# A two-layer hybrid trunk: first tiles and weights in a fixed order of need, keys and values tile by tile, the end-of-layer scaling on VectorE

## The chip, the cores and the metric

The kernel runs on one core of a Trainium2 chip. The metric is the time of one execution in microseconds (us) on the device; less is better. The text calls the engines as the profile does: PE (TensorE, matrix products), PEld (its weight loads), DVE (VectorE), ACT (ScalarE), POOL (GpSimd) and SP (SyncE, which issues the transfers). Each engine works through its own list of instructions in order, so an instruction that waits holds up everything behind it on its engine.

## What is computed

Two layers, each of this form, on x of 512 x 1024 in float32:

```
h    = rms_norm(x, g_pre)
proj = h @ w_in         # q_h, f_h, i_h, z_h (1024 each), q_a (1024), k_a, v_a (128 each), z_a (1024)
o_h  = hgrn2(q_h, f_h, i_h, lb)              # gated linear recurrence, 8 heads, state 128 x 128
o_h  = rms_norm(o_h, g_head) * silu(z_h)
q_a, k_a = rotary(q_a), rotary(k_a)          # 16 query heads, 2 key heads of 64
o_a  = sliding_window_attention(q_a, k_a, v_a, sinks) * silu(z_a)   # window 128
y    = concat(o_h, o_a) @ w_out              # 2048 -> 1024
x    = x + rms_norm(y, g_post)
```

## The kernel before

The tokens are four tiles of 128 (`NT`). Every projection is done with three products in a reduced-precision float format (`mm3`): each operand is split into a rounded part (`hi`) and the rest (`lo`), and a product is hi x lo, lo x hi and hi x hi, added in one PSUM tile.

Weights come in pieces of 128 x 512. SP loads a piece (`raw`, three buffers), ACT rounds it to `whi` (L169; `wkv` for the keys' and values' weights), and DVE takes the difference, `wlo` (L170). For every second piece of the slabs in `POOL_SLABS` and of the keys and values it is POOL that makes `wlo`. `w_conv` runs ahead of use by a count of pieces.

The projections are slabs of 512 columns, in a fixed order: `kv` (256 columns), `QA` and the next one (attention queries; the text calls the second QA+1), `IV` and so on, and at the end the output slabs up to `h1`. A slab is a row of units, each one PSUM tile with its steps over k (a step is one `mm3`, three matmuls). `step()` takes one step, in turn from one or two active units: when the only active one is half done, the next is begun beside it. Work that belongs to a later step is put into a list with `later(steps, key, fn)`, counted down by one at each step; `ensure(key)` runs it at once when a unit needs it. `merge` runs the streams of attention and recurrence between the steps.

At the start of a layer `pre_norm` makes each tile's mean square (ACT, L302), the inverse root `r` (one DVE and one POOL operation, `rstd2`, L280 and L282), `xn` (DVE, L306, two halves), eight transposes on PE (L311), and by `split_psum` the rounded part `hhi` (ACT, L267) and the rest `hlo` (DVE, L268). A `kv` unit's eviction copies its PSUM tile on ACT, rotates the keys on DVE at once, writes the values `vst`, and defers the key transposes by 16 steps. The QA evictions write `rot` with DVE (L378 to L385), POOL (L388, L389), ACT (L391) and DVE again; SP stores it as `stack` and loads it back as `qs`.

At the end of a layer (`final`, from L733 on) each half of `y` is added up on DVE (L719), squared on ACT (L745), its first half multiplied by g_post on POOL (L747, `y<-y,b`), the second on DVE (L750), then `r`, and `a` is the new x (L753, two halves). In layer 1 `pre_norm` of the next layer follows with `defer` of `DEFER` = 18 steps.

The order of instructions on each engine is made by a scheduler from the order in the code and from priorities (`tc.high_priority`); `pin` keeps an instruction in the place it was written.

Of the kernel before, what the change touches and what calls it, by code (L numbers as in the profile page):

```python
# [19 lines left out]
DEPTH = 2  # L20
# [17 lines left out]
LEAD = 4  # L38
POOL_SLABS = (QA,)
# [26 lines left out]
def hybrid_kernel(ctx: ExitStack, tc: tile.TileContext, x, wkv, win, wout, g_pre, g_post, lbp, ghead, sinks,  # L66
# [80 lines left out]
    def w_load(n):  # L147
        while state["raw"] < min(n, len(pieces)):
            i = state["raw"]
            src = pieces[i]  # L150
            t = wp.tile([P, 512], F32, tag="raw", name="raw", bufs=RAW_BUFS)
            nc.sync.dma_start(t.rearrange("p (a c) -> p a c", a=2) if len(src.shape) == 3 else t, src)
            raws[i] = t
            state["raw"] += 1

    def w_conv(n):
        w_load(n)
        while state["conv"] < min(n, len(pieces)):
# [5 lines left out]
            if i in kv_pieces:  # L164
                hi, lo = (big.tile([P, 512], F32R, tag="v", name="wkv", bufs=8) for _ in range(2))
            else:
                hi = wp.tile([P, 512], F32R, tag="whi", name="whi")
                lo = wp.tile([P, 512], F32R, tag="wlo", name="wlo")
            nc.scalar.copy(hi, v)  # L169
            (nc.gpsimd if i in on_pool and i % 2 else nc.vector).tensor_tensor(lo, v, hi.bitcast(F32), op=ALU.subtract)  # L170
            conv[i] = (hi, lo)
# [39 lines left out]
    def step():  # L211
        if not active or (len(active) == 1 and units and 2 * (len(active[0].ks) - active[0].i) <= len(active[0].ks)):
# [64 lines left out]
    def rstd2(ss):  # L277

        t = sm.tile([P, 1], F32, tag="s1", name="s1")
        nc.vector.scalar_tensor_tensor(t, ss[:, 0:1], EPS, ss[:, 1:2], op0=ALU.add, op1=ALU.add)  # L280
        r = sm.tile([P, 1], F32, tag="r1", name="r1")
        nc.gpsimd.tensor_tensor(r, t, mhalf[:, 0:1], op=ALU.pow)  # L282
        return r
# [12 lines left out]
    def pre_norm(tt, xt, g, hT, key, defer=0):  # L296

        ss = sm.tile([P, 2], F32, tag="ss", name="ss")
        xn2 = big.tile([P, 2, 512], F32, tag="q", name="xn", bufs=QB)
        for c in range(2):  # L300
            junk = tmp("u")
            nc.scalar.activation(junk, xt[c], AF.Square, scale=1.0 / 32.0, accum_out=ss[:, c:c + 1])  # L302
        r = rstd2(ss)
        for c in range(2):
            xn = xn2[:, c]
            nc.vector.scalar_tensor_tensor(xn, xt[c], r, g[c], op0=ALU.mult, op1=ALU.mult)  # L306

            def rest(c=c, xn=xn):
                o = sc()
                for j in range(4):  # L310
                    pin(nc.tensor.transpose(o[:, j * P:(j + 1) * P], xn[:, j * P:(j + 1) * P], ident))  # L311
                ov = o.rearrange("p (k t) -> p k t", k=4)
                sl = (slice(None), slice(4 * c, 4 * c + 4), slice(tt * P, (tt + 1) * P))
                split_psum(hT[0][sl], hT[1][sl], ov)

            later(defer, key if c == 1 else None, rest)
            if not defer:
                run_first()
# [5 lines left out]
    def layer(l, last):  # L324
# [4 lines left out]
        def kv_evac(tt, o):  # L329
# [10 lines left out]
            k4 = raw[:, 0:128].rearrange("p (v d) -> p v d", v=2)  # L340
            x1, x2 = k4[:, :, 0:32], k4[:, :, 32:64]
            cb = kcos[:, tt, :].unsqueeze(1).broadcast_to([P, 2, 32])
            sb = ksin[:, tt, :].unsqueeze(1).broadcast_to([P, 2, 32])
            kk = rk[:, 256:512].rearrange("p (v d) -> p v d", v=2)
            m = sm.tile([P, 4, 2, 32], F32, tag="km", name="km", bufs=1)
            nc.vector.tensor_tensor(m[:, 0], x1, cb, op=ALU.mult)
            nc.vector.tensor_tensor(m[:, 1], x2, sb, op=ALU.mult)
            nc.vector.tensor_tensor(m[:, 2], x2, cb, op=ALU.mult)
            nc.vector.tensor_tensor(m[:, 3], x1, sb, op=ALU.mult)
            nc.vector.tensor_tensor(kk[:, :, 0:32], m[:, 0], m[:, 1], op=ALU.subtract)  # L350
            nc.vector.tensor_tensor(kk[:, :, 32:64], m[:, 2], m[:, 3], op=ALU.add)
            nc.scalar.copy(kk[:, :, 64:128], kk[:, :, 0:64])
# [9 lines left out]
            later(16, ("k", l, tt), rest)  # L362
# [348 lines left out]
        def wo_stream(b, s, final=None):  # L711
            def evac(o, tt, ch):
# [4 lines left out]
                else:  # L717
                    with tc.high_priority(200 if final else 0):
                        nc.vector.tensor_tensor(yt[tt][:, ch], o, yt[tt][:, ch], op=ALU.add)  # L719
                if final is not None:  # L720
                    final(tt, ch)
# [10 lines left out]
        def final(tt, ch):  # L732
# [11 lines left out]
            junk = tmp("u")  # L744
            nc.scalar.activation(junk, y[:, ch], AF.Square, scale=1.0 / 32.0, accum_out=ss[:, ch:ch + 1])  # L745
            if ch == 0:
                nc.gpsimd.tensor_tensor(y[:, 0], y[:, 0], hT2["gpost"][0], op=ALU.mult)  # L747
# [38 lines left out]
    def x_tile(tt):  # L786
        t = halves("a") if tt < 2 else (lambda v: [v[:, 0], v[:, 1]])(big.tile([P, 2, 512], F32, tag="oy", name="x0", bufs=6))
        for c in range(2):
            nc.sync.dma_start(t[c], x[tt * P:(tt + 1) * P, c * 512:(c + 1) * 512])
        return t  # L790
# [6 lines left out]
    gpre = load_g(g_pre[0])  # L797
    w_load(1)
    for tt in range(1, NT):
        xts.append(x_tile(tt))  # L800
        w_load(1 + tt)
# [3 lines left out]
    for _ in range(6):  # L805
        nc.tensor.matmul(warm, lhsT=zero[:, 0:P], rhs=zero, start=True, stop=True)
    hT[0] = new_hT()
    for tt in range(NT):
# [100 lines left out]
```

## Time and profile before

| what | value |
|---|---|
| time, median of 3 runs | 962.07 us (960.97 to 962.83) |
| the profiled execution | 959.31 us, its span 957.6 us |
| PE busy | 921.2 us (96%) |
| DVE, ACT, POOL busy | 683.7, 478.4, 268.9 us |
| mean granted PE clock | 0.986 |
| weight pieces rounded on ACT, `whi` | 256, 0.62 us each |
| pieces with `wlo` on DVE / POOL | 248 / 8, and 4 / 4 of the keys and values |

The table is from the page of the profile. A row of the timeline or of the groups gives the start (timeline only), the time, engine, line, operation, output<-inputs, shape, and in brackets the engine's idle time just before and what ended it. In a row of waits stand the total in us, how many, and the longest. In a row of windows stand the stretch, its length, the busy time of PE, PEld, DVE, ACT and POOL with their counts, then the granted PE clock (1.00 is full speed), the share of the DMA engines and GB/s.

### The profile page before, as it was taken

Reading aid. Unit: us, or ns where it says so; the run is one execution under the profiler, and the core shown is the slowest. Engines: PE = TensorE matmul, PEld = TensorE weight load, DVE = VectorE, ACT = ScalarE, POOL = GpSimd, SP = SyncE. Lnnn points to the kernel's source line nnn. Section 1 sums busy time; section 2 is a strip of 40 time slices with the busy share of each in tenths; the row PEclk is TensorE's granted clock in tenths of the full one; section 3 lists DMA queues with packets and bytes.
Section 4 is the critical chain, followed back from the end, with each engine's and each line's share of the span. In section 5 each row is a group of like instructions: output and inputs, shape, how many; then the busy total and the mean of one; then the engine's idle time right before and its main releaser. Section 6 shows DMA issues by size and latency. Waiting matters only on the chain.

```text
span 957.6 us, 19092 instructions
## 1 busy us (share of the span) xinstructions
PE 921.2 (96%) x7228; PEld 757.5 (79%) x7228; DVE 683.7 (71%) x1382; ACT 478.4 (50%) x1135; POOL 268.9 (28%) x282
## 2 busy tenths in 40 slices
PE   7999999999999999999979998999999999999996
PEld 5888777777878888788868886877788887887885
DVE  5766888786757785765794678878867568849546
ACT  5434656836545462334552365676374545514242
POOL 2322454422231221211231234434322213113102
PEclk9999999999999999999989999999999999999998
DMA  6366433122413343324452775112223123513313
GB/s 227 101 197 201 137 81 89 52 71 67 122 46 89 90 132 89 107 71 112 133 163 66 198 209 155 34 56 88 79 58 98 55 79 100 155 51 107 88 45 132
DMA packets 56716, 101.34 MB, mean 106 GB/s; under 512 B 6448, under 2 KB 8880, under 8 KB 56624
## 3 DMA queue, kind: packets, MB, share of 16 engines
q1 hardware_dynamic: 56624, 100.12, 35.1%
q8 instruction: 57, 0.93, 0.4%
q14 instruction: 35, 0.29, 0.1%
HBM read 87.52 MB, written 12.58 MB: 105 GB/s over the span
## 4 chain that ended last, share of the span: by engine, by line
PE 78%; DVE 11%; ACT 6%; issue 2%; POOL 2%; DMA 1%; SPq 0%; DVEq 0%; POOLq 0%; ACTq 0%
PE pj L175 22%; PE pj L177 22%; PE pj L176 21%; DVE wlo L170 3%; PE sc L583 2%; PE sc L428 2%; PE ac L652 1%; ACT s L442 1%; PE ac L655 1%; PE ac L640 1%; DVE oa L487 1%; PE ac L481 1%; DVE q L600 1%; PE sc L455 1%; PE sc L700 1%
## 5 line engine op out<-in xcount | busy, mean ns | idle before, releaser
L169 ACT CAST whi<-raw 128x512 fp32r<-128x512 f32 x256 | 157.2, 621 | 131.2 <-PE pj L177 61.0
L170 DVE TENSOR_TENSOR wlo<-raw,whi 128x512 fp32r<-128x512 f32 x248 | 190.1, 778 | 44.8 <-ACT whi L169 42.4
L175 PE MATMUL pj<-hhi,wlo 128*128 128x512 f32 x512 | 206.0, 402 | 0.0
L177 PE MATMUL pj<-hhi,whi 128*128 128x512 f32 x512 | 200.1, 391 | 0.0
L176 PE MATMUL pj<-hlo,whi 128*128 128x512 f32 x512 | 199.5, 390 | 0.0
L177 PEld LDWEIGHTS pj<-hhi,whi 128*128 128x128 f32 x512 | 96.1, 188 | 21.0
L175 PEld LDWEIGHTS pj<-hhi,wlo 128*128 128x128 f32 x512 | 96.2, 188 | 18.6
L176 PEld LDWEIGHTS pj<-hlo,whi 128*128 128x128 f32 x512 | 96.3, 188 | 18.0
L175 PE MATMUL pj<-whi,ops 128*128 128x512 f32 x256 | 103.8, 406 | 0.0
L175 PE MATMUL pj<-whi,hlo 128*128 128x512 f32 x256 | 103.0, 405 | 0.0
L176 PE MATMUL pj<-wlo,hhi 128*128 128x512 f32 x256 | 102.1, 399 | 0.0
L177 PE MATMUL pj<-whi,hhi 128*128 128x512 f32 x256 | 101.4, 396 | 0.0
L177 PE MATMUL pj<-whi,ops 128*128 128x512 f32 x256 | 100.1, 391 | 0.0
L176 PE MATMUL pj<-wlo,ops 128*128 128x512 f32 x256 | 99.7, 390 | 0.0
L601 POOL TENSOR_TENSOR k<-k,tot 128x256 f32<-128x256 f32 x80 | 66.0, 844 | 109.5 <-PE sc L583 60.5
L600 DVE TENSOR_TENSOR q<-q,tot 128x256 f32<-128x256 f32 x80 | 48.3, 629 | 14.5 <-PE sc L594 7.6
L442 ACT ACTIVATE s<-sc,negm 128x128 f32<-128x128 f32 x128 | 45.6, 370 | 25.7 <-DVE negm L436 25.4
L449 POOL TENSOR_TENSOR s<-s,sums 128x512 f32<-128x512 f32 x32 | 34.4, 1074 | 83.4 <-DVE sums L447 47.9
L177 PEld LDWEIGHTS pj<-whi,hhi 128*128 128x128 f32 x256 | 48.9, 191 | 10.2
L177 PEld LDWEIGHTS pj<-whi,ops 128*128 128x128 f32 x256 | 48.0, 188 | 10.7
L176 PEld LDWEIGHTS pj<-wlo,hhi 128*128 128x128 f32 x256 | 49.2, 192 | 8.4
L175 PEld LDWEIGHTS pj<-whi,hlo 128*128 128x128 f32 x256 | 48.8, 191 | 8.6
(172 smaller groups left out, 1594.8 us busy)
## 6 DMA issues: line engine op xcount, KB each, us to landing
raw<-in_win_dram SPq DMA_DIRECT2D x192, 256.0 KB, 2.7
raw<-in_wout_dram SPq DMA_DIRECT2D x64, 256.0 KB, 2.7
stack<-rot SPq DMA_DIRECT2D x16, 512.0 KB, 4.4
qs<-stack SPq DMA_DIRECT2D x32, 256.0 KB, 5.0
a<-in_x_dram SPq DMA_DIRECT2D x12, 256.0 KB, 2.9
raw<-in_wkv_dram SPq DMA_DIRECT2D x8, 256.0 KB, 4.0
x_mid<-a SPq DMA_DIRECT2D x8, 256.0 KB, 2.1
a<-x_mid SPq DMA_DIRECT2D x8, 256.0 KB, 2.9
```

The costliest lines, as they stand in the source:

```text
L169: nc.scalar.copy(hi, v)
L170: (nc.gpsimd if i in on_pool and i % 2 else nc.vector).tensor_tensor(lo, v, hi.bitcast(F32), op=ALU.subtract)
L175: nc.tensor.matmul(o, lhsT=sta[1], rhs=mov[0], start=start, stop=False)
L176: nc.tensor.matmul(o, lhsT=sta[0], rhs=mov[1], start=False, stop=False)
L177: nc.tensor.matmul(o, lhsT=sta[0], rhs=mov[0], start=False, stop=stop)
L428: pin(nc.tensor.matmul(S[:, h * 256:(h + 1) * 256], lhsT=q[:, 2 * hp_ + h, t_], rhs=kst[v][p][:, (n - 1) * P:(n + 1) * P], start=(h == 0 a ...
L442: nc.scalar.activation(pt[:, h * P:(h + 1) * P], cur[h], AF.Exp, bias=negm[:, h:h + 1], scale=SCALE, accum_out=sums[:, h:h + 1])
L449: nc.gpsimd.tensor_tensor(pv, pv, sums.unsqueeze(2).broadcast_to([P, 4, P]), op=ALU.mult)
L455: pin(nc.tensor.transpose(T[:, h * P:(h + 1) * P], pt[:, h * P:(h + 1) * P], ident))
L583: pin(nc.tensor.matmul(L[32 * b:32 * b + 32, c:c + 16], lhsT=k[:, o_:o_ + 32], rhs=qv[:, blk:blk + qu, 1, :], start=True, stop=True, tile_ ...
L600: nc.vector.tensor_tensor(qv[:, :, 1, :], qv[:, :, 1, :], tv[:, :, 0].unsqueeze(2).broadcast_to([P, nb, hh]), op=ALU.mult)
L601: nc.gpsimd.tensor_tensor(kv_[:, :, 0, :], kv_[:, :, 0, :], tv[:, :, 1].unsqueeze(2).broadcast_to([P, nb, hh]), op=ALU.mult)
```

## The change

1. Start of the kernel: the x tiles are one transfer of 512 KB each in place of two; the first weight piece goes ahead of g_pre and `ident`; the fourth goes to a spare buffer (`z0`); the key tables come before the small constants and three pieces of `QA`, and `masks` after four of these and the rotary tables. The constants are prepared after 26 steps (`constants`, by `later`).
2. `first_norm` replaces `pre_norm` in the first layer: squares, norms, transposes, splits and the first four weight splits in a pinned order written by hand.
3. Four warm-up matmuls in place of six.
4. `kv` units are not begun beside another unit.
5. The keys' rotation (`turn`) is deferred by 16 steps, and the transposes by 16 more.
6. POOL no longer makes `wlo` of the keys' and values' weights, nor of the first half of `QA`.
7. `y<-y,b` moves from POOL to DVE; `final` and the split in `pre_norm` run at high priority (`CHAIN` = 200).

```diff
         for key, (first, n) in slab_first.items():
-        if key[0] == "kv" or key[2] in POOL_SLABS:
-            on_pool.update(range(first, first + n))
+        if key[0] == "in" and key[2] in POOL_SLABS:
+            on_pool.update(range(first + n // 2, first + n))
...
+    ahead["kv", 0] = KT // 2 - LEAD - 2
...
-            t = wp.tile([P, 512], F32, tag="raw", name="raw", bufs=RAW_BUFS)
+            t = tmp("z0") if i == RAW_BUFS else wp.tile([P, 512], F32, tag="raw", name="raw", bufs=RAW_BUFS)
...
-        if not active or (len(active) == 1 and units and 2 * (len(active[0].ks) - active[0].i) <= len(active[0].ks)):
+        if not active or (len(active) == 1 and units and units[0].key[0] != "kv" and 2 * (len(active[0].ks) - active[0].i) <= len(active[0].ks)):
...
-            def rest(c=c, xn=xn):
-                o = sc()
...
+            def rest(c=c):
+                with tc.high_priority(CHAIN):
+                    split_psum(place(hT[0], tt, c), place(hT[1], tt, c), turned(xn, c))
...
+        sq(0, 0), sq(0, 1), rs(0), whi(0), xn(0), wlo(0)
+        hi(0, 0), whi(1), hi(0, 1), lo(0, 0), wlo(1), lo(0, 1)
+        sq(1, 0), whi(2), sq(1, 1), wlo(2), rs(1), whi(3), wlo(3), xn(1)
+        sq(2, 0), sq(2, 1)
+        def second():
+            hi(1, 0), lo(1, 0), hi(1, 1), lo(1, 1), rs(2), xn(2), sq(3, 0), sq(3, 1)
+        def third():
+            hi(2, 0), lo(2, 0), hi(2, 1), lo(2, 1), rs(3), xn(3)
+        def fourth():
+            hi(3, 0), lo(3, 0), hi(3, 1), lo(3, 1)
+        emitted.add(("h", 0, 0))
+        for tt, fn in ((1, second), (2, third), (3, fourth)):
+            later(8 * tt - 2, ("h", 0, tt), fn)
...
+            def turn():
...
+                later(16, ("k", l, tt), rest)
-            later(16, ("k", l, tt), rest)
+            later(16, None, turn)
...
-                    final(tt, ch)
+                    with tc.high_priority(CHAIN):
+                        final(tt, ch)
...
-                nc.gpsimd.tensor_tensor(y[:, 0], y[:, 0], hT2["gpost"][0], op=ALU.mult)
+                nc.vector.tensor_tensor(y[:, 0], y[:, 0], hT2["gpost"][0], op=ALU.mult)
...
     xts = [x_tile(0)]
+    w_load(1)
+    gpre = load_g(g_pre[0])
     ident = const_tile(ident_c, [P, P], F32, "ident")
...
-    for tt in range(1, NT):
-        xts.append(x_tile(tt))
-        w_load(1 + tt)
+    xts.append(x_tile(1))
+    w_load(3)
+    xts.append(x_tile(2))
+    w_load(4)
+    xts.append(x_tile(3))
...
-    for _ in range(6):
+    for _ in range(4):
         nc.tensor.matmul(warm, lhsT=zero[:, 0:P], rhs=zero, start=True, stop=True)
...
+    later(26, None, constants)
```

Where the scheduler then puts the instructions is seen in their order on each engine. Three places follow, each as it stands before and now.

DVE at the start. `s` is the sum under the root, `r` its inverse root, `km` the products of the key rotation. Before:

```order
L280 SCALAR_TENSOR_TENSOR s_126<-ss 128x1
L170 TENSOR_TENSOR wkv<-raw,wkv 128x512
L306 SCALAR_TENSOR_TENSOR xn<-a,r_128,b 128x512 x2
L280 SCALAR_TENSOR_TENSOR s_150<-ss 128x1
L306 SCALAR_TENSOR_TENSOR xn<-a,r_152,b 128x512
L268 TENSOR_TENSOR hlo<-sc_79,hhi 128x4x128
L268 TENSOR_TENSOR hlo<-sc_80,hhi 128x4x128
```

Now the first rows and, in the second fence, the rows up to tile 3's `hlo`:

```order
L282 SCALAR_TENSOR_TENSOR s_127<-ss 128x1
L307 SCALAR_TENSOR_TENSOR xn<-a,r_129,b 128x512 x2
L363 TENSOR_TENSOR wkv<-raw,wkv 128x512
L356 TENSOR_TENSOR hlo<-sc_79,hhi 128x4x128
L363 TENSOR_TENSOR wkv<-raw,wkv 128x512
L356 TENSOR_TENSOR hlo<-sc_80,hhi 128x4x128
L363 TENSOR_TENSOR wkv<-raw,wkv 128x512
```

```order
L307 SCALAR_TENSOR_TENSOR xn<-x_103,r_299,b 128x512 x2
L173 TENSOR_TENSOR wlo<-raw,whi 128x512
L894 CAST masks<-u 128x512
L901 TENSOR_TENSOR lb_mx<-lp 128x8
L425 TENSOR_TENSOR s<-km 128x2x32
L903 TENSOR_TENSOR lb_e<-lp,lb_mx 128x8 x2
L173 TENSOR_TENSOR wlo<-raw,whi 128x512
L356 TENSOR_TENSOR hlo<-sc_79,hhi 128x4x128
L356 TENSOR_TENSOR hlo<-sc_80,hhi 128x4x128
```

The weight split has moved behind the first tile's `xn`, and the cast of the masks stands ahead of the last tile's `hlo`.

ACT in the QA slabs of the first layer (`kst` are the transposed keys). Before and now:

```order
L352 COPY s<-s 128x2x64
L365 CAST vst<-s 128x64
L267 CAST kst<-sc_80 128x128 x2
L267 CAST kst<-sc_78 128x128 x2
L391 CAST rot<-rot 128x512 x2
L169 CAST whi<-raw 128x512 x8
L391 CAST rot<-rot 128x512 x4
L169 CAST whi<-raw 128x512 x5
L391 CAST rot<-rot 128x512 x2
```

```order
L458 CAST rot<-rot 128x512 x2
L172 CAST whi<-raw 128x512 x2
L269 CAST kst<-sc_80 128x128 x2
L172 CAST whi<-raw 128x512 x4
L269 CAST kst<-sc_78 128x128 x2
L458 CAST rot<-rot 128x512 x2
L172 CAST whi<-raw 128x512 x2
L458 CAST rot<-rot 128x512 x2
L172 CAST whi<-raw 128x512 x5
L458 CAST rot<-rot 128x512 x2
```

Before the first `rot` pair stand nine `whi` in both. The second pair stood behind eight more, and stands now behind six; two `whi` follow it. The same holds in layer 2.

DVE at the layer boundary, with tile 1's `xn` in the first row of the one and the fourth of the other. Before and now:

```order
L306 SCALAR_TENSOR_TENSOR xn<-a,r_5318,b 128x512 x2
L280 SCALAR_TENSOR_TENSOR s_5361<-ss 128x1
L170 TENSOR_TENSOR wlo<-raw,whi 128x512
L753 SCALAR_TENSOR_TENSOR a<-y,r_5363,a 128x512
L719 TENSOR_TENSOR y<-pj,y 128x512
L753 SCALAR_TENSOR_TENSOR a<-s,r_5363,a 128x512
L268 TENSOR_TENSOR hlo<-sc_78,hhi 128x4x128
L719 TENSOR_TENSOR y<-pj,y 128x512
```

```order
L173 TENSOR_TENSOR wlo<-raw,whi 128x512
L282 SCALAR_TENSOR_TENSOR s_5309<-ss 128x1
L817 TENSOR_TENSOR s<-y,b 128x512
L307 SCALAR_TENSOR_TENSOR xn<-a,r_5311,b 128x512 x2
L814 TENSOR_TENSOR y<-y,b 128x512
L282 SCALAR_TENSOR_TENSOR s_5355<-ss 128x1
L270 TENSOR_TENSOR hlo<-sc_78,hhi 128x4x128
L820 SCALAR_TENSOR_TENSOR a<-y,r_5357,a 128x512
L820 SCALAR_TENSOR_TENSOR a<-s,r_5357,a 128x512
L270 TENSOR_TENSOR hlo<-sc_79,hhi 128x4x128
```

Tile 0's first `hlo` has moved ahead of the two `a`, and `y<-y,b` stands ahead of it.

More of the change, by code (lines that the diff above doesn't have):

```diff
@@ L154, in w_load, with w_parts @@
             state["raw"] += 1
+    def w_parts(i):
+        if i in kv_pieces:
+            return tuple(big.tile([P, 512], F32R, tag="v", name="wkv", bufs=8) for _ in range(2))
+        return (wp.tile([P, 512], F32R, tag="whi", name="whi"), wp.tile([P, 512], F32R, tag="wlo", name="wlo"))
     def w_conv(n):
@@ L163, in w_conv @@
             v = raws.pop(i)
[L164 to L168, printed above, removed]
+            conv[i] = hi, lo = w_parts(i)
             nc.scalar.copy(hi, v)
             (nc.gpsimd if i in on_pool and i % 2 else nc.vector).tensor_tensor(lo, v, hi.bitcast(F32), op=ALU.subtract)
-            conv[i] = (hi, lo)
             state["conv"] += 1
@@ L293, in load_g, with squares, new_xn, scaled @@
         return t
[L296 removed]
+    def squares(v, ss, c):
+        return nc.scalar.activation(tmp("u"), v, AF.Square, scale=1.0 / 32.0, accum_out=ss[:, c:c + 1])
+    def new_xn():
+        return big.tile([P, 2, 512], F32, tag="q", name="xn", bufs=QB)
+    def scaled(xn, xt, r, g, c):
+        return nc.vector.scalar_tensor_tensor(xn[:, c], xt[c], r, g[c], op0=ALU.mult, op1=ALU.mult)
+    def turned(xn, c):
+        o = sc()
+        for j in range(4):
+            pin(nc.tensor.transpose(o[:, j * P:(j + 1) * P], xn[:, c, j * P:(j + 1) * P], ident))
+        return o.rearrange("p (k t) -> p k t", k=4)
```

163 lines of the change are left out of this document (87 added, 76 removed).

## The prediction

> **What bounds the kernel now.** I read the page first, then the waits of PE, then the stretches at a lower clock, and then the places the change touches.
>
> ```profile
> span 957.6 us, 19092 instructions
> PE 921.2 (96%) x7228; PEld 757.5 (79%) x7228; DVE 683.7 (71%) x1382; ACT 478.4 (50%) x1135; POOL 268.9 (28%) x282
> PE 78%; DVE 11%; ACT 6%; issue 2%; POOL 2%; DMA 1%; SPq 0%; DVEq 0%; POOLq 0%; ACTq 0%
> ...
> PE pj L175 <- DVE hlo L268: 6.6, 2, 5.7
> ...
> PE sc L311 <- DVE xn L306: 3.2, 2, 2.0
> ...
> 484.49:491.31 6.82, 5.50 (x26) 5.51 (x27) 6.58 (x11) 4.58 (x12) 2.73 (x4) 0.50 0.47 154
> 593.71:597.13 3.42, 1.69 (x9) 1.11 (x9) 2.77 (x6) 1.20 (x7) 0.91 (x1) 1.00 1.06 233
> 597.13:600.54 3.41, 3.41 (x15) 3.12 (x15) 2.66 (x7) 1.87 (x6) 1.04 (x1) 0.50 0.36 132
> ```
>
> PE is busy for 96% of the span and carries 78% of the chain that ends last. The change removes none of its large matmuls, so it can move only PE's idle time, some 36 us (957.6 less 921.2), and the stretches at clock 0.50. The waits that it aims at are the wait of 5.7 us for `hlo` at the layer boundary and the first layer's start. The window rows (stretch, then busy time by engine, then the granted clock) show what a wait costs besides: in 593.71 to 597.13 PE was busy for 1.69 of 3.42 us, and the next 3.41 us ran at 0.50.
>
> [...]
>
> **The start.** x and weights land in another order, the first layer's DVE and ACT work is in a fixed order, POOL no longer makes `wlo` of the keys' and values' weights (L170), and one keys-and-values unit runs at a time.
>
> ```profile
> b<-in_g_pre_dram SPq DMA_DIRECT2D x2, 256.0 KB, 4.9
> 2.16 0.91 SPq L292 DMA_DIRECT2D b<-in_g_pre_dram  x2
> ...
> 9.22 0.69 DVE L170 TENSOR_TENSOR wkv<-raw,wkv 128x512 fp32r<-128x512 f32 x1 [4.14 <-ACT wkv L169]
> 9.83 1.41 DVE L306 SCALAR_TENSOR_TENSOR xn<-a,r,b 128x512 f32<-128x512 f32 x2
> 11.34 1.27 POOL L170 TENSOR_TENSOR wkv<-raw,wkv 128x512 fp32r<-128x512 f32 x1 [5.63 <-ACT wkv L169]
> 13.16 0.75 DVE L306 SCALAR_TENSOR_TENSOR xn<-a,r,b 128x512 f32<-128x512 f32 x1 [1.85 <-POOL r L282]
> 13.96 1.11 PE L311 MATMUL sc<-ident,xn 128*128 128x128 f32 x4 [2.02 <-DVE xn L306]
> 14.73 0.56 PE L175 MATMUL pj<-wkv,hlo 128*128 128x256 f32 x1
> 30.43 0.40 PE L175 MATMUL pj<-hhi,wlo 128*128 128x512 f32 x1
> ...
> L268 DVE TENSOR_TENSOR hlo<-sc,hhi 128x512 fp32r<-128x512 f32 x16 | 10.7, 681 | 0.4 <-ACT hhi L267 0.4
> L282 POOL TENSOR_TENSOR r<-s,mhalf x16: 539/546/926, 5.2 to 952.4; 128x1 f32<-128x1 f32 x16
> ```
>
> Before, the first norm stands behind a weight split that waits 4.14 us, the second waits for `r` behind POOL's 1.27 us, and the first real matmul starts at 14.73. In the new order tile 0's `xn` is ahead of the weight split, so it is gated by g_pre alone: issued by 3.07 and 4.9 us underway, it is there near 8.0 to 8.4, not 9.83. With the transposes and the `hhi` between, the first `hlo` starts near 9.7 and the keys and values near 10.4 (both 1.4 us less than 9.83 would give). That is some 4 us earlier, but it isn't the end of the stage: that is where the QA matmuls begin, at 30.43. From the first `hlo` to the one before tile 3's, DVE has in the new order 6 `hlo`, 6 `xn`, 3 weight splits of keys and values, 5 `wlo` and some 17 small ones: with 0.08 us of each row overlapped, 6 x 0.60 + 6 x 0.67 + 8 x 0.60 + 17 x 0.13 = 14.6 us. To it come three waits of 0.6 us for `r` (0.55 by the row, with the hand-overs) and one for `masks`, whose cast now stands ahead of tile 3's `hlo` on DVE and waits for a transfer moved behind four weight pieces and two tables: 0 to 2.5 us. So tile 3's first `hlo` ends at 9.7 + 14.6 + 1.8 + 0.7 = 26.8 to 29.3, and its 24 matmuls, 0.12 us apart as 502.87 and 502.99 below, bring QA to 29.7 to 32.2. Against 30.43 that is -0.7 to +1.8; I take +0.4, since a transfer moved back is likelier late than not. What was a wait of PE before becomes waits between tiles, one at a time and with nothing interleaved. The deferred constants and the `wlo` that POOL gave up are among the DVE rows just counted (in layer 2 DVE has slack for two more `wlo`: it is busy for 71%). The two warm-up matmuls fewer, and keys that are turned 16 steps later but read only in attention, I cost at nothing; what covers the first is a PE that waits for data there anyway, and without that cover it is a cold window (the second rival).
>
> **QA and QA+1, in both layers.** The deferred key rotation moves the steps at which ACT meets the rotated queries. `rot` casts (L391 before, L458 after) now stand ahead of the last `whi` of QA+1 and the first of IV; before, they stood behind both.
>
> ```profile
> 57.68 0.62 ACT L169 CAST whi<-raw 128x512 fp32r<-128x512 f32 x1 [0.56 <-DMA raw<-in_win_dram]
> 63.12 0.62 ACT L391 CAST rot<-rot 128x512 fp32r<-128x512 f32 x1 [2.27 <-POOL rot L389]
> 57.76 0.68 DVE L384 TENSOR_TENSOR rot<-pj,cs 128x512 f32<-128x512 f32 x1
> 58.36 0.68 DVE L170 TENSOR_TENSOR wlo<-raw,whi 128x512 fp32r<-128x512 f32 x1
> 60.67 0.67 DVE L385 TENSOR_TENSOR rot<-pj,cs 128x512 f32<-128x512 f32 x1
> 58.52 1.67 POOL L388 TENSOR_TENSOR rot<-rot 128x512 f32<-128x512 f32 x1 [10.06 <-DVE rot L384]
> 61.42 1.67 POOL L389 TENSOR_TENSOR rot<-rot 128x512 f32<-128x512 f32 x1 [1.23 <-DVE rot L385]
> 60.82 0.39 PE L175 MATMUL pj<-hhi,wlo 128*128 128x512 f32 x1
> ```
>
> The matmul at 60.82 is the 127th large one, the eighth step of QA+1's first unit, and the first to read the eighth `wlo` of QA+1. Before, that `wlo` was made at 58.36, 1.78 us ahead of its use (60.82 less 59.04). In the new order its `whi` waits for both POOL rotations. DVE can run L385 right behind L384, at 58.36, so POOL does both back to back: 58.52 + 2 x 1.30 to 1.67 = 61.1 to 61.9; the second cast (0.62), then `whi` (0.62), then `wlo` (0.69) end at 63.0 to 63.8. PE waits 2.2 to 3.0 us where it had none; a rotation that starts earlier against PE, as with a full DVE just before, brings that down to 1.5. I take 2.1 a layer, **+4.2** for both. Below it could be 0, if the first unit of QA+1 reaches its eighth piece later than here.
>
> **Attention.** The same shift of steps reorders DVE's small operations and weight splits.
>
> ```profile
> 119.89 3.92 DVE L170 TENSOR_TENSOR wlo<-raw,whi 128x512 fp32r<-128x512 f32 x3
> 125.44 1.40 PE L417 MATMUL sc<-kst,qs 128*128 128x128 f32 x8 [1.73 <-ACT s L442]
> ```
>
> Three `wlo` in a row took 3.92 us there in place of 1.9 (`wlo` is 0.68 alone), PE waited 1.73 us afterwards, and its clock fell to 0.50. In the new order the three are spread over the block. A gain up to this wait and a cold window, 1.73 + 1.7 = 3.4 a layer (half of 3.41 is lost in a cold window), against a loss as large where another reduction is now late: I take -0.5 a layer, **-1.0**.
>
> **The layer boundary.** POOL's `y<-y,b` (L747) becomes DVE's, and `hlo` gets priority.
>
> ```profile
> 479.71 0.39 PE L177 MATMUL pj<-whi,ops 128*128 128x512 f32 x1
> 485.81 0.58 PE L175 MATMUL pj<-wkv,hlo 128*128 128x256 f32 x1 [5.71 <-DVE hlo L268]
> 502.87 0.28 PE L177 MATMUL pj<-wkv,hhi 128*128 128x256 f32 x1
> 502.99 0.39 PE L175 MATMUL pj<-hhi,wlo 128*128 128x512 f32 x1
> 478.61 2.44 DVE L306 SCALAR_TENSOR_TENSOR xn<-a,r,b 128x512 f32<-128x512 f32 x2 [0.44 <-POOL r L282]
> 485.07 0.68 DVE L268 TENSOR_TENSOR hlo<-sc,hhi 128x512 fp32r<-128x512 f32 x1
> 478.54 1.29 POOL L747 TENSOR_TENSOR y<-y,b 128x512 f32<-128x512 f32 x1
> ```
>
> Before, the last output matmul starts at 479.71 and QA of layer 2 at 502.99: 23.28 us. `hlo` of tile 0 starts 6.46 us after tile 1's `xn` (485.07 less 478.61), which took 2.44 us in place of 1.4 beside POOL's `y<-y,b`. In the new order only two `xn`, `y<-y,b` on DVE and one small operation stand between: 2.1 us. So 4.3 us of the 5.71 go, and more as nothing holds the `xn`: tile 0 waits 0.3 to 1.4. Late next is tile 1. Between tile 0's `hlo` and tile 1's second stand on DVE thirteen operations, 8.4 us by the same rows, against 3.7 us of PE work on tile 0 (24 x 0.12, and some 0.9 for eight transposes, of which four took 1.11 at half clock in the row of 13.96): PE waits some 5.0 there, 0.9 to 2.5 for tile 2, 0.4 for tile 3. With no overlap of tiles the stage is 0.3 + 2.8 + 0.9 + 5.0 + 3.7 + 1.7 + 3.7 + 0.4 + 2.8 = 21.3 us, **-2.0**. The bounds are +0.5 (the 5.0 makes a cold window) and -3.5 (tile 1 waits 3.5).
>
> [...]
>
> **The end.**
>
> ```profile
> 949.04 1.39 DVE L719 TENSOR_TENSOR y<-pj,y 128x512 f32<-128x512 f32 x2
> 949.82 0.63 ACT L745 ACTIVATE u<-y 128x512 f32<-128x512 f32 x1 [3.33 <-DVE y L719]
> 951.33 0.96 DVE L280 SCALAR_TENSOR_TENSOR s<-ss 128x1 f32<-128x1 f32 x1 [0.17 <-ACT u L745]
> 952.95 0.75 DVE L753 SCALAR_TENSOR_TENSOR a<-y,r,a 128x512 f32<-128x512 f32 x1 [0.66 <-POOL r L282]
> ```
>
> After the change `y<-y,b` stands on DVE between the two evictions, and it must wait for the square of the first half (949.82, 0.63 us and the read of its sum, to 950.64). The tile before ends the same way and pushes 949.04 to about 949.4. Then: square done 951.0, `y<-y,b` to 951.6 (0.68, as the `wlo` above, which has the same operands), second eviction 952.1, its square 952.9, `s` 953.0, `r` 953.7, `a` at 953.8 in place of 952.95: **+0.85**. The bounds are +1.3 (the lateness of all four tiles adds up) and -0.8 (nearly all of the 0.96 us of `s`, one number per partition).
>
> **The sum** against the profiled run (span 957.6 and 1.71 around it): 959.31 + 0.4 + 4.2 - 1.0 - 2.0 + 0.85 = 961.8. That run lies 2.76 under the median, 962.07, so against the median it is 962.07 + 2.45 = **964.5 us**, slower by 0.25%. A change within 0.2% (1.9 us) can't be told from none.
>
> **Rivals.**
> - Faster. The order on ACT costs nothing, because QA+1's eighth piece is used after the casts, and the boundary loses its wait and its cold stretch: 0.4 - 1.0 - 3.5 + 0.3 = -3.8, and with a warm attention block in each layer to -7: 955 to 958. For it speaks that the two waits of the profile named above (5.7 and 2.0) are really removed from their places; against it the ACT order. It decides at 1.8 us: if the second rotation's cast ends less than that much later than 58.3, PE never sees it.
> - Slower by more. Each wait of 2.1 us falls into one window, as in 593.71 to 597.13, and halves the next: 1.7 more a layer; the sparse start, with no second tile interleaved, is cold for another two windows (+2): 964.5 + 3.4 + 2 = 970. For it: 1.7 us of idle was enough. Against: a wait that straddles two windows doesn't.
> - No change. The QA wait is 1.5 and attention and boundary gain what their rows allow (-1.5 and -2.5): 3.0 + 0.4 - 1.5 - 2.5 + 0.8, rounded +0.2: 962.3.
>
> [...]
>
> **The numbers.** The sum as it stands 0.38, the faster rival 0.27, the slower 0.18, no change 0.17. The sum's own range is 962 to 967, and a third of it lies within 0.2%. So faster 0.27, same 0.17 + 0.12 = 0.29, slower 0.26 + 0.18 = 0.44. The range for all, 956 to 970, takes in both outer rivals but for their far ends.
>
> **What would show it.** In the new profile: the first keys-and-values matmul near 10.4 and QA at 29.7 to 32.2; a PE wait of 1.5 to 3 us for DVE `wlo` near 62 and near 533, which was not in the list; at the boundary the wait of 5.7 gone, one of some 5 for `hlo` of tile 1, and 21.3 us from last output matmul to QA; the end 0.85 longer from the last matmul. The prediction is wrong if PE doesn't wait for `wlo` in QA+1, or if tile 1 at the boundary is ready when tile 0 is done.

## The result, and the profile after

The changed kernel takes 970.01 us (median of 4 runs, 969.75 to 971.72) against 961.55 us before (4 runs on the same chip): the ratio on record is 1.0098, with a 95% interval of 1.0083 to 1.0113 (the quotient of these two medians is 1.0088). It is slower by 8.5 us. Forecast were 964.5 us, slower by 2.45, with a range up to 970.0: the sign was right, the size was less than a third, and the time fell just outside the range.

The page of the changed kernel, and the waits of PE (total in us, times, longest):

```profile
span 968.1 us, 19074 instructions
PE 920.7 (95%) x7224; PEld 754.5 (78%) x7224; DVE 684.0 (71%) x1398; ACT 476.7 (49%) x1135; POOL 246.7 (25%) x266
...
PE pj L177 <- DVE hlo L270: 6.0, 2, 5.0
PE pj L177 <- DVE wlo L173: 5.6, 2, 3.2
PE pj L177 <- DVE hlo L356: 4.8, 4, 2.3
```

PE is as busy as before (920.7 and 921.2 us); the span has grown by 10.5 us, and by the sums all of it is idle time. The sums hide the clock: as shown below, two windows at half clock are new in QA+1, and the three that the kernel before had in attention are gone. The wait for `wlo` was not in the list of the kernel before at all. The wait for `hlo` is nearly as long as before (longest 5.0 and 5.7), but for another tile. The first lines of each stage let the loss be placed; they are PE's rows, to be set against 30.43, 479.71 and 502.99 before:

```profile
11.10 0.51 PE L177 MATMUL pj<-wkv,hlo 128*128 128x256 f32 x1 [0.83 <-DVE hlo L356]
29.73 0.38 PE L177 MATMUL pj<-wkv,hlo 128*128 128x256 f32 x1 [2.25 <-DVE hlo L356]
31.63 0.40 PE L177 MATMUL pj<-hhi,wlo 128*128 128x512 f32 x1
64.89 0.50 PE L177 MATMUL pj<-hhi,wlo 128*128 128x512 f32 x1 [2.42 <-DVE wlo L173]
...
483.19 0.39 PE L179 MATMUL pj<-whi,ops 128*128 128x512 f32 x1
493.55 0.58 PE L177 MATMUL pj<-wkv,hlo 128*128 128x256 f32 x1 [4.95 <-DVE hlo L270]
505.94 0.40 PE L177 MATMUL pj<-hhi,wlo 128*128 128x512 f32 x1
540.07 0.65 PE L177 MATMUL pj<-hhi,wlo 128*128 128x512 f32 x1 [3.18 <-DVE wlo L173]
957.95 0.39 PE L179 MATMUL pj<-whi,ops 128*128 128x512 f32 x1
```

| stretch | forecast, us | measured, us |
|---|---|---|
| start, to the first QA matmul | +0.4 | +1.2 (31.63 against 30.43) |
| QA and QA+1, layer 1 | +2.1 | +4.6 |
| rest of layer 1 (attention, recurrence, output) | -0.5 | -2.3 |
| last output matmul to QA of layer 2 | -2.0 | -0.5 (22.75 against 23.28) |
| QA and QA+1, layer 2 | +2.1 | +5.5 |
| rest of layer 2 up to the last large matmul | -0.5 | +0.2 |
| last large matmul to the end | +0.85 | +1.8 (10.1 against 8.3) |
| sum | +2.45 | +10.5 in the two profiled runs |

The rows inside the layers are found by comparing the start of the same large matmul, counted from the first, in both traces. The QA rows end at the 141st (63.99 before and 69.80 after) and at the 1681st (537.49 and 545.90). The profiled run of before lies 2.2 us under its median, so 8.5 of the 10.5 us remain in the medians.

Nearly the whole loss lies in one place, taken twice. Windows (stretch, length, busy time of PE, PEld, DVE, ACT and POOL, granted PE clock) of the changed kernel stand behind the rows of ACT and DVE in layer 1 and of POOL in both layers; the last two windows are of the kernel before:

```profile
61.65 0.62 ACT L458 CAST rot<-rot 128x512 fp32r<-128x512 f32 x1 [0.91 <-POOL rot L455]
62.89 0.62 ACT L458 CAST rot<-rot 128x512 fp32r<-128x512 f32 x1 [0.62 <-POOL rot L456]
63.41 1.13 ACT L172 CAST whi<-raw 128x512 fp32r<-128x512 f32 x2
62.30 1.93 DVE L459 TENSOR_TENSOR rot<-rot 128x512 fp32r<-128x512 f32 x2 [1.07 <-ACT rot L458]
64.15 1.29 DVE L173 TENSOR_TENSOR wlo<-raw,whi 128x512 fp32r<-128x512 f32 x2
60.32 1.30 POOL L455 TENSOR_TENSOR rot<-rot 128x512 f32<-128x512 f32 x1 [10.62 <-DVE rot L451]
535.53 1.30 POOL L455 TENSOR_TENSOR rot<-rot 128x512 f32<-128x512 f32 x1 [11.47 <-DVE rot L451]
...
62.40:65.82 3.42, 1.00 (x5) 0.80 (x5) 2.90 (x4) 1.66 (x3) 0.46 (x1) 1.00 0.77 162
65.82:69.23 3.41, 3.41 (x10) 2.61 (x9) 1.29 (x2) 0.00 (x0) 0.00 (x0) 0.50 0.87 308
492.49:499.31 6.82, 5.76 (x27) 5.76 (x28) 6.38 (x16) 3.33 (x8) 2.63 (x2) 0.50 0.77 251
536.85:540.27 3.42, 0.24 (x2) 0.20 (x2) 2.63 (x4) 2.27 (x4) 1.20 (x1) 1.00 0.98 226
540.27:543.69 3.42, 3.42 (x9) 2.67 (x9) 1.64 (x3) 0.00 (x0) 0.00 (x0) 0.50 0.64 222
...
105.62:109.03 3.41, 3.41 (x12) 2.73 (x10) 2.50 (x6) 1.80 (x10) 3.01 (x4) 0.50 0.10 39
126.09:129.50 3.41, 3.41 (x14) 3.02 (x13) 2.98 (x7) 1.84 (x4) 1.04 (x1) 0.50 0.25 90
```

This is the chain of the forecast link by link: ACT waits for POOL's second rotation, casts it at 62.89, and only then makes QA+1's eighth `whi`; its `wlo` starts at 64.15 and PE goes on at 64.89. DVE's own `rot` pair stands ahead of that `wlo` too, but it hardly matters: it ends at 64.23, when the `whi` has ended at 64.03 (63.41 and 0.62), and so it costs some 0.1 us. The wait of layer 1, 2.42 us, lies within the 2.2 to 3.0 of the forecast. In layer 2 it is 3.18: POOL's first rotation began 1.36 us before PE ran out of work there (535.53, and 540.07 less 3.18), and 2.15 us before in layer 1 (60.32, and 64.89 less 2.42). What the price left out is the clock. In both layers the window that holds the wait (PE busy for 1.00 and 0.24 of 3.42 us) was followed by one at clock 0.50. Half clock is not new as such: the kernel before had it in attention, in the last two rows and in 597.13 to 600.54 of the prediction, where the profile of the changed kernel has none. The row of 492.49 is the boundary's, behind the wait for tile 1; the kernel before had such a stretch there too (484.49 to 491.31).

### The profile page after: what moved, and what is told of

It is laid out like the page before. It is cut to its first block, busy times and chain, and to the rows that moved or that the text cites. A ratio compares the mean times of both kernels' runs of the same rounds, so it can differ in the third digit from the quotient of the medians.

```text
span 968.1 us, 19074 instructions
## 1 busy us (share of the span) xinstructions
PE 920.7 (95%) x7224; PEld 754.5 (78%) x7224; DVE 684.0 (71%) x1398; ACT 476.7 (49%) x1135; POOL 246.7 (25%) x266
## 4 chain that ended last, share of the span: by engine, by line
PE 71%; DVE 14%; ACT 6%; issue 3%; POOL 3%; DMA 2%; SPq 0%; DVEq 0%; POOLq 0%; ACTq 0%
PE pj L177 21%; PE pj L179 20%; PE pj L178 19%; DVE wlo L173 3%; PE sc L495 2%; PE sc L650 2%; ACT s L509 2%; PE ac L719 1%; DMA raw<-in_win_dram 1%; DVE oa L554 1%; PE ac L722 1%; PE ac L707 1%; ACT whi L172 1%; PE ac L548 1%; POOL r L284 1%
## 5 line engine op out<-in xcount | busy, mean ns | idle before, releaser
L178 PE MATMUL pj<-wlo,hhi 128*128 128x512 f32 x256 | 100.1, 391 | 0.0
L179 PEld LDWEIGHTS pj<-whi,ops 128*128 128x128 f32 x256 | 48.0, 188 | 10.7
L177 PEld LDWEIGHTS pj<-whi,ops 128*128 128x128 f32 x256 | 48.1, 188 | 9.7 <-DVE ops L770 0.3
L178 PEld LDWEIGHTS pj<-wlo,ops 128*128 128x128 f32 x256 | 48.2, 188 | 8.9
```

The lines of the kernel that those rows point to most:

```text
L177: nc.tensor.matmul(o, lhsT=sta[1], rhs=mov[0], start=start, stop=False)
L178: nc.tensor.matmul(o, lhsT=sta[0], rhs=mov[1], start=False, stop=False)
L179: nc.tensor.matmul(o, lhsT=sta[0], rhs=mov[0], start=False, stop=stop)
```

## The experiments

Each is told with the median of its runs, and the ratio to the kernel before on the same chip with its 95% interval. Across runs of one kernel the median of before lay between 960.7 and 961.6 us.

**Key transposes earlier (e1_rest_soon).** ACT's order in QA+1 hangs on when the key transposes are written, not on the rotation: with 1 step between rotation and transposes, ACT has eight `whi` between the first and second `rot` pair again, as before the change.

```diff
-                later(16, ("k", l, tt), rest)
+                later(1, ("k", l, tt), rest)
```

> The changed kernel with the key transposes 1 step after the keys' rotation in place of 16 (so 17 steps after the unit's end, not 32); the rotation stays deferred. ACT then has the eighth whi of QA+1 ahead of the second rot pair again, in both layers. Theory (the order on ACT makes the two PE waits for wlo, and each wait halves the next clock window): both waits (2.4 and 3.2 us) and both cold windows (1.7 each) go, 970.0 - 9.0 = 961 (959 to 963.5). Rival A (waits only, the clock fell for another reason): -5.6, 964.4. Rival B (the loss sits in the start, the boundary and the end, and PE would wait there for something else): 968 to 970.

961.64 us, ratio 1.0010 (0.9994 to 1.0025): the kernel is back at the time of before. No wait for `wlo` is left in its list:

```profile
PE pj L177 <- DVE hlo L270: 6.0, 2, 4.9
PE sc L495 <- ACT s L509: 4.2, 5, 1.3
```

and ACT has the `whi` before the casts (rows of ACT, the last `whi` at 58.86):

```profile
58.86 0.63 ACT L172 CAST whi<-raw 128x512 fp32r<-128x512 f32 x1 [0.83 <-DMA raw<-in_win_dram]
60.02 0.62 ACT L458 CAST rot<-rot 128x512 fp32r<-128x512 f32 x1 [0.53 <-POOL rot L455]
62.92 0.62 ACT L458 CAST rot<-rot 128x512 fp32r<-128x512 f32 x1 [2.28 <-POOL rot L456]
```

One number of the change, 16 steps, carries nearly the whole loss: 8.4 of the 8.5 us by the medians. What is left of the change then neither gains nor loses by the medians.

**The deferral alone, on the kernel before (e2_before_late_turn).**

```diff
-            later(16, ("k", l, tt), rest)
+            def turn():
+                ...                       # the rotation, as it stood above
+                later(16, ("k", l, tt), rest)
+            later(16, None, turn)
```

> The kernel before with part 5 alone: the keys' rotation 16 steps later and the transposes 16 steps after that. ACT has the second rot pair ahead of QA+1's eighth whi, as in the changed kernel. Theory: this part alone makes a PE wait of 2 to 3.5 us for wlo in QA+1 in each layer and a cold window behind it, +8.5, less up to 3 us if the shift of steps also takes the cold windows out of layer 1's attention: 961.5 + 5.5 to 9 = 967 to 970.5. Rival (it takes the tile-by-tile keys and values as well to bring the order to bear): 961 to 963, no wait of over 1 us for wlo.

965.41 us, ratio 1.0051 (1.0036 to 1.0066), below the expected 967. The waits came as told. The windows, below them, hold the wait of layer 1 and what followed it:

```profile
64.77 0.50 PE L175 MATMUL pj<-hhi,wlo 128*128 128x512 f32 x1 [2.51 <-DVE wlo L170]
537.86 0.80 PE L175 MATMUL pj<-hhi,wlo 128*128 128x512 f32 x1 [3.12 <-DVE wlo L170]
...
59.55:62.96 3.41, 2.71 (x12) 1.90 (x11) 2.35 (x5) 1.08 (x3) 2.53 (x2) 1.00 0.83 243
62.96:66.37 3.41, 1.60 (x7) 1.34 (x8) 2.82 (x5) 1.46 (x3) 0.00 (x0) 1.00 0.71 143
66.37:69.79 3.42, 3.42 (x17) 2.83 (x16) 0.69 (x2) 0.00 (x0) 0.00 (x0) 1.00 0.74 282
```

So the part needs no other part to do harm. The loss of 4.7 us is less than the two waits, 5.6 us. The profile shows two reasons. The wait of layer 1 falls into two windows, and full clock follows it; half clock follows only the wait of layer 2 (537.44 to 540.86). And none of the three windows at half clock that attention had in the profile before is left, as the expectation allowed for layer 1 (the mean granted clock is 0.990 against 0.986). Whether the latter is the deferral's doing or chance is not settled.

**Half the deferral (e3_half_late).** With 24 steps in all, the order is the old one in layer 1 and the new one in layer 2.

```diff
-            later(16, None, turn)
+            later(8, None, turn)
```

> The changed kernel with the rotation 8 steps after the unit's end (24 to the transposes). The ACT order in QA+1 is then the good one in layer 1 and the bad one in layer 2. Theory: the PE wait near 64 us and its cold window go (-2.4 - 1.7 = -4.1), the ones near 540 us stay: 966 (964.5 to 967.5). Rival A (waits only): -2.4, 967.6. Rival B (order on ACT irrelevant): 969.5 to 970.5, or both waits gone or both there.

963.86 us, ratio 1.0033 (1.0018 to 1.0048). One wait is left, the second:

```profile
534.14 0.50 PE L177 MATMUL pj<-hhi,wlo 128*128 128x512 f32 x1 [3.10 <-DVE wlo L173]
```

The wait goes exactly where the order goes. The time fell by 6.2 us and not by 4.1: in its profile the rest of layer 1 was shorter as well, 411.5 us against 413.4. Neither profile has a window at half clock there, and why it was shorter is open.

**POOL at the end (e4_pool_at_end).** `y<-y,b` goes back to POOL in the last layer only.

```diff
-                nc.vector.tensor_tensor(y[:, 0], y[:, 0], hT2["gpost"][0], op=ALU.mult)
+                (nc.gpsimd if last else nc.vector).tensor_tensor(y[:, 0], y[:, 0], hT2["gpost"][0], op=ALU.mult)
```

> The changed kernel with y<-y,b back on POOL in the last layer only (layer 1 keeps it on DVE). Theory (at the end DVE is the bound, 5.84 us a tile against 5.45 us of PE, since y<-y,b waits for the square between the two evictions): the 1.9 us that the stretch from the last large matmul to the end grew by go again but for the collision of POOL with s: 968.3 (967.8 to 969.0), last large matmul to end of span 8.3 us in place of 10.1. Rival (the collisions with POOL cost as much): 969.5 to 970.5.

966.60 us, ratio 1.0069 (1.0052 to 1.0085): 3.4 us less than the changed kernel, twice what was expected. From its last large matmul (954.87) to the end of its span (963.1) it takes 8.3 us, as before the change. The changed kernel's end shows why (DVE rows):

```profile
952.94 0.68 DVE L786 TENSOR_TENSOR y<-pj,y 128x512 f32<-128x512 f32 x1
954.47 0.69 DVE L814 TENSOR_TENSOR y<-y,b 128x512 f32<-128x512 f32 x1 [0.85 <-ACT u L301]
958.76 0.68 DVE L786 TENSOR_TENSOR y<-pj,y 128x512 f32<-128x512 f32 x1
963.25 0.75 DVE L820 SCALAR_TENSOR_TENSOR a<-y,r,a 128x512 f32<-128x512 f32 x1 [0.66 <-POOL r L284]
```

DVE stands still for 0.85 us in each tile, for ACT's square, and needs 5.82 us a tile (952.94 to 958.76), PE 5.45 (24 matmuls 0.227 apart). The other 1.6 us of the gain do not come from the end. Up to there each engine has its instructions in the same order as in the changed kernel, but in this profile the waits in QA+1 are shorter, and no window at half clock is behind them. The windows below hold the second wait and what followed it:

```profile
66.93 0.50 PE L177 MATMUL pj<-hhi,wlo 128*128 128x512 f32 x1 [2.06 <-DVE wlo L173]
538.85 0.50 PE L177 MATMUL pj<-hhi,wlo 128*128 128x512 f32 x1 [2.10 <-DVE wlo L173]
...
537.01:540.43 3.42, 1.58 (x7) 1.30 (x8) 2.82 (x5) 1.50 (x3) 0.00 (x0) 1.00 0.68 152
540.43:543.84 3.41, 3.41 (x17) 2.80 (x16) 0.72 (x2) 0.00 (x0) 0.00 (x0) 1.00 0.75 277
```

The first wait falls into two windows (the border is at 65.96). Of the second 1.84 us lie in one window, in which PE was busy for 1.58 us, and even so full clock follows.

**Both repairs (f1_both).** Transposes after 1 step, POOL at the end.

> The changed kernel with the key transposes 1 step after the rotation (as e1_rest_soon) and y<-y,b on POOL in the last layer (as e4_pool_at_end). Theory (the two losses, the waits for wlo in QA+1 and DVE as the bound at the end, are separate and add up): 961.6 - 1.8 = 959.8 (959.0 to 960.8), last large matmul to end 8.3 us. Rival (they overlap, or one of the two kernels gained by chance of clock windows): 961 to 962.5.

961.20 us, ratio 1.0004 (0.9993 to 1.0015), not the 959.8 of a sum. Its instructions stand in the same order as in the first experiment up to the last layer's end, and that end is 1.8 us shorter in its profile. But the two profiles differ in attention (f1_both, then e1_rest_soon):

```profile
103.40:106.86 3.46, 1.49 (x10) 1.28 (x10) 3.41 (x8) 1.87 (x10) 2.53 (x3) 1.00 0.77 292
106.86:110.27 3.41, 3.41 (x12) 2.73 (x11) 2.42 (x7) 0.67 (x4) 3.01 (x4) 0.50 0.00 0
...
103.40:106.86 3.46, 1.50 (x9) 1.36 (x10) 3.41 (x8) 1.87 (x11) 2.61 (x3) 1.00 0.72 273
106.86:110.27 3.41, 3.26 (x19) 2.54 (x18) 3.24 (x8) 1.21 (x5) 3.01 (x4) 1.00 0.02 5
```

The same work, with PE busy for 1.5 of 3.46 us, was followed by half clock in one run and by full clock in the other. In these traces the windows at half clock start a whole number of times 3.413 us apart: in the changed kernel at 11.21, 65.82, 492.49 and 540.27, which is 16, 125 and 14 times; in the kernel before at 13.45, 105.62, 126.09, 484.49 and 597.13, which is 27, 6, 105 and 33 times; in f1_both at 106.86 and 127.34, which is 6 times. Against the program this grid lies elsewhere in each: a border stands at 105.62 in the kernel before, at 106.78 in the changed kernel, at 106.86 in f1_both and at 107.12 in e1_rest_soon. By its own grid f1_both has the window 103.45 to 106.86 with PE busy for 1.44 us, and e1_rest_soon the window 103.71 to 107.12 with 1.76 us. The busy share alone is no sharp bound in these profiles: in f1_both the window 123.93 to 127.34, busy for 1.83 us, was followed by half clock, and the one of 1.58 us in e4_pool_at_end was not. Windows that come and go so are a likely reason why runs of one kernel spread over 3 to 6 us where ten or more were taken (e1_rest_soon: 958.65 at a mean granted clock of 0.991 to 964.66 at 0.985), and why two medians of ten and eleven runs can hide 1.8 us. The end was therefore weighed again on a steadier kernel, below.

**Overlap of keys and values again (f2_overlap):** part 4 undone, on f1_both.

```diff
-        if not active or (len(active) == 1 and units and units[0].key[0] != "kv" and 2 * ...
+        if not active or (len(active) == 1 and units and 2 * ...
```

> As f1_both, with part 4 undone: keys-and-values units are begun beside another unit again. Theory (one unit at a time leaves PE waiting for each tile's hlo, at the start and at the boundary, where a second unit or a QA unit could run): the boundary from last output matmul to QA shrinks by some 2 us, the start by 0 to 2: 956.5 (955 to 959). Rival (the tile-by-tile order is what took the boundary's wait for tile 0 away): 961 to 963.

958.88 us, ratio 0.9973 (0.9963 to 0.9983): 2.3 us less, so tile by tile is a loss by itself. At the boundary its profile waits 1.74 and 3.82 us for `hlo` where that of f1_both waits 1.05, 4.94 and 0.96, which is 1.4 us less. Where the rest lies is not settled.

**The boundary: transposes of the next layer earlier,** on f1_both (g1_defer10) and on f2_overlap (g2_defer10_overlap).

```diff
-DEFER = 18
+DEFER = 10
```

> As f1_both, with DEFER 10 in place of 18: the next layer's transposes and hlo are written 10 steps after the norm, and so stand earlier on DVE and PE. Theory (the wait of 4.95 us at the boundary is for tile 1's hlo, which stands on DVE behind the later tiles' ends; put earlier it is covered by the matmuls of h1): the boundary falls from some 22.5 to 14 to 17 us, the two cold windows behind the wait go, the matmuls of h1 lose 1 to 2 us to earlier transposes: 953.5 (951 to 956.5). Rival (DVE is the bound of the whole boundary, some 6.4 us of work a tile against 5.45 us of PE, so order doesn't matter): 959 to 961.

> f2_overlap and g1_defer10 together: overlap of keys-and-values units and DEFER 10. Theory (two separate gains, of which the boundary's share of the overlap is lost since no wait is left there): 952 (949.5 to 955). Rival (each alone takes away the same wait): as g1_defer10, 953 to 956.

955.88 us, ratio 0.9943 (0.9929 to 0.9956), and with the overlap 952.17 us, ratio 0.9907 (0.9894 to 0.9920). PE at the boundary of the latter:

```profile
477.75 0.66 PE L312 MATMUL sc<-ident,xn 128*128 128x128 f32 x4 [0.83 <-DVE xn L307]
482.04 0.39 PE L179 MATMUL pj<-whi,ops 128*128 128x512 f32 x1
491.69 0.66 PE L312 MATMUL sc<-ident,xn 128*128 128x128 f32 x4 [0.42 <-DVE xn L307]
495.65 0.40 PE L177 MATMUL pj<-hhi,wlo 128*128 128x512 f32 x1
```

From the last output matmul to QA it takes 13.6 us (495.65 less 482.04) where it took 22.75: the wait of 4.95 us for tile 1 and both cold windows behind it are gone (between 484 and 497 us most of the keys' and values' matmuls take 0.28 us each, where those behind that wait took 0.41), and the longest wait left in that stretch is 0.42 (0.83 just before it). Part of this is paid for earlier: the transposes of one more tile now stand ahead of the last output matmul, and the rest of layer 1 takes 417.5 us in this profile against 414.7 in that of f1_both. The overlap brought 3.7 us here too, though g1_defer10 without it has hardly a wait at the boundary either (0.69 us in all). So the boundary is not the only place where tile by tile costs; in these two profiles the start differs most, 32.5 against 30.7 us, with one window at half clock in the former and none in the latter (the mean granted clock of the whole is 0.992 and 0.994).

**DEFER 10 alone, on the kernel before (h1_before_defer10).** The edit is the same.

> The kernel before with DEFER 10 in place of 18, and nothing else. Theory (earlier transposes pay only together with part 7, y<-y,b off POOL and hlo at high priority, since without them hlo stands on DVE behind the blocked xn and a): the boundary falls by 0 to 4 us and the matmuls of h1 lose 2 to 5: 961 (959 to 963). Rival (DEFER alone makes the gain of g1_defer10): 954 to 957.

962.39 us, ratio 1.0011 (0.9997 to 1.0024): nothing is gained. In its trace transposes wait up to 3.9 us for `xn` at the boundary (and h2_pool_boundary below gains although it has `y<-y,b` on POOL, so this operation is not all that stands in the way):

```profile
494.72 1.12 PE L311 MATMUL sc<-ident,xn 128*128 128x128 f32 x4 [3.92 <-DVE xn L306]
```

**POOL at the boundary too (h2_pool_boundary), and DVE at the end (h4_dve_end),** both on g2_defer10_overlap: `y<-y,b` on POOL in both layers, or on DVE in both.

```diff
-                (nc.gpsimd if last else nc.vector).tensor_tensor(y[:, 0], ...)
+                nc.gpsimd.tensor_tensor(y[:, 0], ...)     # h2
+                nc.vector.tensor_tensor(y[:, 0], ...)     # h4
```

> g2_defer10_overlap with y<-y,b on POOL in both layers. Theory (at the boundary DVE's own 0.69 us is the smaller price: POOL's 1.29 us blocks xn and a, as in the kernel before): the boundary grows by 3 to 5 us: 956 (954.5 to 957.5). Rival (DVE is the bound there and is relieved of 0.6 us a tile): 950 to 952.5.

> g2_defer10_overlap with y<-y,b on DVE in the last layer too, as in the changed kernel. It measures the price of DVE at the end on a kernel with few cold windows. Theory: +1.8 us, 954.0 (953.4 to 954.6), last large matmul to end 10.1 in place of 8.3. Rival (f1_both gained only 0.4 over e1_rest_soon because the end costs less over many runs than in one profile): 952.2 to 953.

956.67 us, ratio 0.9946 (0.9926 to 0.9966), and 953.84 us, ratio 0.9922 (0.9906 to 0.9937). By the medians that is +4.5 and +1.7 us against the base, by the ratios, which allow for another chip, +3.8 and +1.4. DVE at the boundary, in h2 and then in the base:

```profile
469.40 2.46 DVE L307 SCALAR_TENSOR_TENSOR xn<-a,r,b 128x512 f32<-128x512 f32 x2 [0.67 <-POOL r L284]
...
469.10 1.41 DVE L307 SCALAR_TENSOR_TENSOR xn<-a,r,b 128x512 f32<-128x512 f32 x2 [0.67 <-POOL r L284]
```

The first stands beside POOL's `y<-y,b` (469.37, 1.27 us), and the boundary takes 16.1 us in h2's profile where it takes 13.6 in the base. The rest of h2's loss is not placed: its profile has four windows at half clock in attention where the base has two (mean granted clock 0.988 against 0.994), which can be chance. The interval of h4 overlaps that of the base a little, but the traces bear it out: from the last large matmul to the end it is 10.0 to 10.1 us in all four profiles with `y<-y,b` on DVE there, and 8.2 to 8.5 in all ten with POOL. So part 7 is right at the boundary and wrong at the end.

**Constants behind the last tile's `hlo` (h3_const30),** on g2_defer10_overlap.

```diff
-    later(26, None, constants)
+    later(30, None, constants)
```

> g2_defer10_overlap with the constants written after 30 steps, not 26, which puts lb_mx and the rest behind tile 3's hlo on DVE (lb_mx took 1.26 us between its two halves there). Theory: the last tile's hlo comes 1.3 us earlier, the start 0.3 to 1.3 us shorter: 951.3 (950.5 to 952.2). Rival (PE is covered by QA there): 952.2, no change.

951.35 us, ratio 0.9896 (0.9875 to 0.9916), the fastest of all. That it beats the base by 0.8 us agrees with the 1.26 us that `lb_mx` took between the two `hlo` there: in its profile `lb_mx` takes 0.15, and QA begins at 29.75 in place of 30.72. But the two intervals overlap.

## Why the prediction was right in sign and wrong in size

- Start: the first keys-and-values matmul came at 11.10 (forecast near 10.4) and QA at 31.63 (29.7 to 32.2, taken: 30.8). Each tile had its wait, the last one 2.25 us. The `masks` transfer was no part of it, since the cast did not wait: the largest part of the delay was `lb_mx` behind it, 1.28 us beside a POOL operation (`wlo`, 26.77, 1.40 us) in place of 0.16 in the kernel before. Parts 1, 2, 3 and 6 were not tried one by one.
- QA and QA+1: the mechanism, the place and the victim were right, and so was its repetition in layer 2. This is the term that was mis-sized: 2.1 us a layer was forecast, 4.6 and 5.5 were measured. The waits were sized well in layer 1 (2.42 us, within the 2.2 to 3.0) and 1.1 us too small in layer 2 (3.18). The step that failed is the one from a wait to its price: the text priced the window at half clock at 1.7 us a layer and then kept it out of the sum, as a rival of 0.18, and it came in both layers of the profile. So of the 5.9 us by which the two rows missed, the windows are 3.4 (an estimate: half of two times 3.41) and the longer waits 1.4; some 0.5 a layer is left, of which 0.3 is there in e1_rest_soon too, without a wait or a cold window. The condition named there, that the wait falls into one window, fits both layers of the changed kernel, and the first wait of e2_before_late_turn, which falls into two windows and cost no half clock (2.51 us, then clock 1.00); that it isn't enough by itself, e4_pool_at_end shows (PE busy for 1.58 of 3.42 us, then clock 1.00).
- Attention: -0.5 a layer was forecast for the new order of DVE. What was measured, -2.3 and +0.2, holds two windows at half clock fewer in layer 1 (105.62 and 126.09) and one fewer in layer 2 (597.13). Such windows come and go with one and the same order (layer 1 has two of them in f1_both and none in e1_rest_soon, and takes 414.7 and 413.1 us), so the term's sign is not settled by these runs.
- Boundary: the wait moved to tile 1 as forecast, 4.95 us against 5.0. Tile 0 still waited 1.03, tiles 2 and 3 not at all: 6.0 us in all, against 6.6 before (5.71 and 0.94). So the waits fell by 0.65 only. The sum of 21.3 us had 7.4 us of waits and its matmuls at full clock, but two windows at half clock stand there now (492.49 to 499.31) as two stood there before (484.49 to 491.31), and by the same estimate they cost 3.4 us. So -0.5 and not -2.0; the bound of +0.5 had this case in it.
- End: DVE was the bound, as said, but each tile takes DVE 5.82 us against PE's 5.45, 0.85 of them standing still, and the lateness of all four adds up: +1.8 and not +0.85, beyond the bound of +1.3 that had this case in it.
- The rivals: "slower by more" is what happened, and the part of it in QA+1 by its own mechanism. That it came to 970 in the text and 970.01 on the chip is luck. Its +2 for a colder start did not come (one window at half clock there before, 13.45 to 16.86, and after, 11.21 to 14.62), and longer waits, the boundary and the end stood in for it. Its chance of 0.18 was too small, since in the trace of before half clock followed the long waits in attention, in both layers (105.62, 126.09 and 597.13, behind windows with PE busy for 1.46, 1.69 and 1.69 us), and at the boundary (484.49, behind one with 0.00).

## What to carry to other kernels

Where an instruction that waits holds up the next on its engine (here ACT's `whi` at 63.41, behind a cast that waited 0.62 us for POOL), a deferral is not free because its own work is off the path: 16 steps on the key transposes let two casts pass the rounding of two weight pieces on ACT, and it cost some 8 us. Read the order of every engine between the moved work and the next weights, and price a wait of PE with the half-clock window that can follow it (here 3.41 us at 0.50 behind waits of 2.42 and 3.18 us), in the sum and not beside it. When a wait is removed at a boundary, ask which tile is late next, and write its work earlier: the same change with its transposes in time (1 step, DEFER 10, overlap kept, POOL at the end) is 1% faster than the kernel before and not 1% slower.

## What the hardware showed that was not expected

Waits of nearly one length were followed by different clocks. In the changed kernel a wait of 2.42 us in QA+1 was followed by 3.41 us at half clock; in e2_before_late_turn a wait of 2.51 us at the same place was followed by none. In e4_pool_at_end, with the order of the changed kernel, the waits were 2.06 and 2.10 us, and none was followed by half clock. And in attention one stretch with PE busy for 1.5 of 3.46 us was followed by clock 0.50 in one run and 1.00 in another, with the same instructions in the same order. The place of the windows against the program differs between these traces (borders at 105.62, 106.78, 106.86 and 107.12), and by the estimate of half a window some 1.7 us hang on it for a long wait. How busy a window must be to keep the clock isn't settled: after 1.44 and 1.83 us of 3.41 (f1_both) and 1.69 (the kernel before) it fell, after 1.58 (e4_pool_at_end), 1.60 (e2_before_late_turn) and 1.76 (e1_rest_soon) it did not.

At its start the changed kernel has one window at half clock, 11.21 to 14.62, at most 1.7 us or 0.2% of the span. The four windows at half clock from there to its last matmul, 65.82, two from 492.49 and 540.27, come to at most 1.7 us each, 0.7% of the span. The kernel before had five such windows between its start and its last matmul (105.62, 126.09, two from 484.49, 597.13), so they do not make the difference in sum; but beside a change of 1% a few windows more or less weigh much.
